# First modulation of the trunk: unsplit float32 products in four column groups instead of split products, with a new opening order

## The chip, the cores and the metric

The kernel runs on one core of one Trainium2 chip. The metric is the device time of one execution in microseconds, the median over repeated executions.

## The reference

A two-layer backbone for a diffusion generator over 256 latent tokens and 256 context tokens of width 1024. Layer 0 mixes tokens with a bidirectional mLSTM, layer 1 with latent attention; each is followed by a gated convolutional feed-forward. Every sub-layer sees its input modulated by six vectors worked out from the condition:

```
m = silu(cond) @ ada_w[i] + ada_b[i]          # (1024) @ (1024, 6*1024), split into six
h = x * (1 + scale) + shift                   # latent tokens: from c, context tokens: from c_ctx
x_m = h @ m_w_up                              # first product of layer 0, (512, 1024) @ (1024, 2048)
```

All of it is float32. The change concerns the first two of the six vectors (shift and scale) of layer 0, for both conditions, and what the first product `x_m` needs of them.

## The kernel before, in words

Large products are made by splitting: a float32 array a is cast on ScalarE to float32r (`hi`), VectorE subtracts (`lo = a - hi`), and TensorE adds three products hi\*hi, hi\*lo, lo\*hi (`mm3`, L405 to L407). Tokens lie along the free axis (512 of them, context first), features on the partitions, in 8 tiles of 128.

The opening (`start_up`) makes the shift and scale of layer 0, modulates the 8 feature tiles, and starts the up projection for its first five column tiles of 128 (`NUP` = 5), which accumulate in five PSUM banks. The rest of the kernel follows from column tile m = 5 on (`w_up`), with weights that a stream loads and splits ahead.

Two lists written out by hand set the order. `LOADS` is the order of the DMAs on SP's queue: `a..` a 128 x 1024 tile of modulation weights (512 KB, 16 in all), `x.` a tile of transposed tokens (256 KB), `w.` a tile of up weights (128 x 640, 320 KB), `s` the small constants. `STEPS` is the order of the work, which is kept as written on TensorE, VectorE and ScalarE:

- `Sgi` splits weight tile i of group g on ScalarE and VectorE (`ada_split`); `Agi` and `Bgi` multiply its high and its low half (`ada_mm`, L487). The stationary operand is `condr`, 4 columns: the high and the low parts of SiLU(c) and SiLU(c_ctx). The result `adar` is a row of 4 partitions.
- `Cg` copies that row out of PSUM on ScalarE (L493), `Tg` transposes it in 128-column pieces to feature-major (`ada_T`, L500), `Og` adds the high and low results and the bias on VectorE into `mod0` (L510, L511).
- `Ek` modulates token tile k, context half on VectorE (L585) and latent half on ScalarE (L587); `Hk` splits the outcome.
- `Wk` splits up weight tile k; `Vkm` adds tile k's contribution to up column tile m, three products of 128x128 by 128x512. There are 40 of these steps.

`GROUPS` says which feature tiles a modulation group holds: 1, 1, 2, 2 and 2. A group of two has products 512 wide, a group of one 256 wide. Ten products on zeros (L627) stand ahead of the first step. `setup` loads the 16 KB with the condition and bias on SP's queue ahead of everything else (L446) and makes `cond` (SiLU, L463) and `condr`.

After the opening the instructions are ordered by the scheduler. The split of column tile 5 goes into a buffer that the up weight tile w3 holds until its last `V3m` step.

Of the kernel before, what the change touches and what calls it, by code (L numbers as in the profile page):

```python
# [7 lines left out]
F32 = mybir.dt.float32  # L8
F32R = mybir.dt.float32r
I32 = mybir.dt.int32  # L10
AF = mybir.ActivationFunctionType
# [38 lines left out]


NUP = 5
GROUPS = ((0, 1), (1, 2), (2, 4), (4, 6), (6, 8))
WARM = 10
LOADS = (
    "a00 a01 a10 a11 a20 a21 x0 w0 x1 a22 a23 w1 s a30 a31 a32 a33 w2 x2 x3 a40 w3 a41 a42 a43 w4 x4 x5 x6 w5 x7 "
    "w6 w7").split()
STEPS = (
# [4 lines left out]
    "V73 V71 V32 V63 V60 V61 V72 V70 V64 V74").split()  # L63

TAIL = {"mout": 4, "aout": 7, "fout1": 6}
WIDE = {"mout": 5, "aout": 7, "fout1": 10}
# [79 lines left out]
def _pack(i):  # L146
# [87 lines left out]

    w0 = np.asarray(i["ada_w"][0]).reshape(8, 128, 6, D)[:, :, 0:2]
    ada0 = []
    for f0, f1 in GROUPS:
        g = w0[..., f0 * 128:f1 * 128].transpose(1, 0, 2, 3).reshape(128, -1)
        ada0 += [g[:, j:j + 1024] for j in range(0, g.shape[1], 1024)]

    up0 = i["m_w_up"][0].reshape(8, 128, -1)[:, :, :NUP * 128]
# [134 lines left out]
class K:  # L376
# [64 lines left out]
    def setup(self):  # L441
        nc, p = self.nc, self.pool
        a = self.a
        self.sm = p.tile([128, a["sm"].shape[1]], F32, name="sm")
        self.sm0 = p.tile([128, NSM0], F32, name="sm0")
        nc.sync.dma_start(self.sm0, a["sm0"])  # L446
        b1 = self.smc("ada_b")[:, 8:16]
        nc.vector.tensor_scalar(b1, b1, 1.0, None, op0=ALU.add)
        jp = p.tile([128, 128], I32, tag="s2", name="jp", bufs=NS)
        nc.gpsimd.iota(jp, pattern=[[1, 128]], base=0, channel_multiplier=-1)  # L450
        self.ident = p.tile([128, 128], F32, name="ident")
        nc.vector.tensor_scalar(self.ident, jp, 0.0, None, op0=ALU.is_equal)
        self.mask = p.tile([128, 2, 128], F32, name="mask")
        nc.vector.tensor_scalar(self.mask[:, 0], jp, 0.0, NEG, op0=ALU.is_gt, op1=ALU.mult)
        nc.vector.tensor_scalar(self.mask[:, 1], jp, 0.0, NEG, op0=ALU.is_lt, op1=ALU.mult)
        self.k1 = p.tile([128, 1], F32, name="k1")
        nc.vector.memset(self.k1, 1.0)
        self.zero = p.tile([128, 512], F32R, tag="s2", name="zero", bufs=NS)
        nc.vector.memset(self.zero.bitcast(F32), 0.0)
        self.keps = p.tile([128, 1], F32, name="keps")  # L460
        nc.vector.memset(self.keps, EPS)
        self.cond = p.tile([128, 8, 2], F32, name="cond")
        nc.scalar.activation(self.cond.rearrange("p a b -> p (a b)"), self.smc("cond"), AF.Silu)  # L463
        self.condr = p.tile([128, 8, 4], F32R, name="condr")
        self.split(self.condr[:, :, 0:2], self.condr[:, :, 2:4], self.cond)
        self.mod0 = p.tile([128, 2, 8, 2], F32, name="mod0")
        self.modc = {(0, c): self.mod0[:, c] for c in range(2)}
        self.gd = {}
        self.adav = p.tile([128, 32], F32, name="adav")
        nc.vector.memset(self.adav, 0.0)  # L470
        for l in range(2):
            for c in (3, 4) if l == 0 else (0, 1, 3, 4):
                self.modc[l, c] = p.tile([128, 8, 2], F32, name="mod%d%d" % (l, c))
            for c in (2, 5):
                self.gd[l, c] = self.dr.tile([2, D], F32, name="gd%d%d" % (l, c))

    def ada_split(self, w):
        hi, lo = [self.pool.tile([128, 1024], F32R, tag="u", name="adas", bufs=NU) for _ in range(2)]
        self.split(hi, lo, w)
        return hi, lo  # L480

    def ada_mm(self, pr, g, i, x, start, stop):

        n = 256 * (GROUPS[g][1] - GROUPS[g][0])
        nk = 1024 // n
        for kk in range(nk):
            self.nc.tensor.matmul(pr[0:4, :n], self.condr[:, i * nk + kk, :], x[:, kk * n:(kk + 1) * n],  # L487
                                  start=start and kk == 0, stop=stop and kk == nk - 1)

    def ada_copy(self, pr, g):  # L490
        r = self.s2("adarow")
        n = 256 * (GROUPS[g][1] - GROUPS[g][0])
        self.nc.scalar.copy(r[0:4, :n], pr[0:4, :n])  # L493
        return r

    def ada_T(self, g, r):
        nf = GROUPS[g][1] - GROUPS[g][0]
        pt = self.ps("adat")
        for i in range(2 * nf):
            self.nc.tensor.transpose(pt[:, 4 * i:4 * i + 4], r[0:4, i * 128:(i + 1) * 128], self.ident[0:4, 0:4])  # L500
        return pt

    def ada_cols(self, g, pt):
        nc = self.nc
        f0, f1 = GROUPS[g]
        nf = f1 - f0
        t = self.tiny(8, "adt")[:, 0:4 * nf].rearrange("p (c f b) -> p c f b", c=2, b=2)
        p = pt[:, 0:8 * nf].rearrange("p (c f b) -> p c f b", c=2, b=4)
        b = self.smc("ada_b").rearrange("p (c f) -> p c f", c=2)[:, :, f0:f1].unsqueeze(3).to_broadcast([128, 2, nf, 2])
        nc.vector.tensor_tensor(t, p[:, :, :, 2:4], b, op=ALU.add)  # L510
        nc.vector.tensor_tensor(self.mod0[:, :, f0:f1, :], p[:, :, :, 0:2], t, op=ALU.add)  # L511

    def ada_bg(self, l, c, k0, k1, nconds):

# [74 lines left out]
    def start_up(self):  # L589
# [10 lines left out]
        for step in LOADS:  # L600
            op, n = step[0], [int(x) for x in step[1:]]
            if op == "a":
                t = raw[step] = self.uf("adaw")
                src = self.a["ada0"][sum(2 * (f1 - f0) for f0, f1 in GROUPS[:n[0]]) + n[1]]
            elif op == "x":
                t = raw[step] = self.s2("xT")
                src = self.a["tokT"][n[0]]
            elif op == "w":
                t = raw[step] = self.pool.tile([128, CW], F32, tag=tag[n[0]][0], name="raw0", bufs=tag[n[0]][1])
                t, src = t[:, :nw], self.a["up0"][n[0]]  # L610
            else:
                t, src = self.sm, self.a["sm"]
            nc.sync.dma_start(t, src)
# [5 lines left out]

        e = mybir.EngineType  # L620
        idle = self.ps("idle")
        rows, parts, hT = {}, {}, {}
        todo = {g: 4 * (f1 - f0) for g, (f0, f1) in enumerate(GROUPS)}
        ps, made = {}, [0] * NUP
        with self.tc.manual_schedule(engines={e.PE, e.DVE, e.Activation}):
            for _ in range(WARM):
                nc.tensor.matmul(idle, self.zero[:, 0:128], self.zero, start=True, stop=True)  # L627
            for step in STEPS:
                op, n = step[0], [int(x) for x in step[1:]]
                g = n[0]  # L630
                if op == "S":
                    parts[g, n[1]] = self.ada_split(raw["a%d%d" % (g, n[1])])
                elif op in "AB":
                    first = g not in rows
                    if first:
                        rows[g] = self.ps("adar")
                    todo[g] -= 1
                    self.ada_mm(rows[g], g, n[1], parts[g, n[1]][op == "B"], first, todo[g] == 0)
                elif op == "C":
                    rows[g] = self.ada_copy(rows[g], g)  # L640
                elif op == "T":
                    rows[g] = self.ada_T(g, rows[g])
                elif op == "O":
                    self.ada_cols(g, rows[g])
                elif op == "E":
                    self.mod_tile(g)
                elif op == "H":
                    h = hT[g] = self.u("hT")
                    self.split(h[:, 0, :], h[:, 1, :], self.xT[g])
                elif op == "W":  # L650
                    if g not in w:
                        w[g] = [self.pool.tile([128, CW], F32R, tag="u", name="w0", bufs=NU) for _ in range(2)]
                    self.split(w[g][0][:, :nw], w[g][1][:, :nw], raw["w%d" % g][:, :nw])
                else:
                    k, m = n
                    if m not in ps:
                        ps[m] = self.ps("up")
                    c = slice(m * 128, (m + 1) * 128)
                    self.mm3(ps[m], (w[k][0][:, c], w[k][1][:, c]), (hT[k][:, 0], hT[k][:, 1]),
                             made[m] == 0, made[m] == 7)  # L660
                    made[m] += 1
        self.hT = [hT[k] for k in range(8)]
        raw = parts = w = w3 = rows = None
        for m in range(NUP):
            self.up_evac(m, ps[m])

# [1351 lines left out]
```

## Time and profile before

| | us |
|---|---|
| median of 3 runs | 1365.69 (1365.69 to 1366.27) |
| span of the profiled execution | 1363.8 |
| TensorE busy in it | 1347.3 |
| VectorE busy | 1073.6 |
| ScalarE busy | 725.3 |
| first up product of the opening starts | 14.90 |
| first product of column tile 5 starts | 53.61 |

The profiled execution is known by its span, from its first to its last instruction; the runs' times also hold what lies around it. Rows of a timeline read: start, length, engine, source line, operation, out<-in with shapes, count, and in square brackets how long the engine was idle before and what ended that. PE is TensorE, PEld its weight loads, DVE VectorE, ACT ScalarE, SPq the DMA queue of SyncE. Grouped rows end with busy time and mean ns of one instruction, then the idle time before them. A TensorE row's length is longer than the distance to the next row's start, since neighbours overlap in the array.

### The profile page before, as it was taken

Reading aid. Unit: us, or ns where it says so; the run is one execution under the profiler, and the core shown is the slowest. Engines: PE = TensorE matmul, PEld = TensorE weight load, DVE = VectorE, ACT = ScalarE, POOL = GpSimd, SP = SyncE. Lnnn points to the kernel's source line nnn. Section 1 sums busy time; section 2 is a strip of 40 time slices with the busy share of each in tenths; the row PEclk is TensorE's granted clock in tenths of the full one; section 3 lists DMA queues with packets and bytes.
Section 4 is the critical chain, followed back from the end, with each engine's and each line's share of the span. In section 5 each row is a group of like instructions: output and inputs, shape, how many; then the busy total and the mean of one; then the engine's idle time right before and its main releaser. Section 6 shows DMA issues by size and latency. Waiting matters only on the chain.

```text
span 1363.8 us, 18639 instructions
## 1 busy us (share of the span) xinstructions
PE 1347.3 (99%) x6605; PEld 1125.5 (83%) x6605; DVE 1073.6 (79%) x1738; ACT 725.3 (53%) x1251; POOL 121.9 (9%) x215
## 2 busy tenths in 40 slices
PE   8999999999999999999999999999999999999997
PEld 5788888888788888888898888888888888888886
DVE  7798656677598696897979978767898789888873
ACT  7765443446544555464643334334557767466660
POOL 0122000010011011030001000000001001000100
PEclk9999999999999999999999999999999999999999
DMA  9788748788666374776627876646998436366750
GB/s 367 273 294 299 272 170 264 228 296 279 216 208 201 101 232 135 249 282 229 210 95 239 301 242 229 219 144 206 307 272 242 142 103 206 114 189 193 257 193 31
DMA packets 92077, 297.60 MB, mean 218 GB/s; under 512 B 12072, under 2 KB 16552, under 8 KB 91984
## 3 DMA queue, kind: packets, MB, share of 16 engines
q1 hardware_dynamic: 62848, 218.52, 48.2%
q0 software_dynamic: 17472, 57.57, 13.5%
q10 hardware_dynamic: 11664, 20.32, 4.1%
q8 instruction: 52, 0.85, 0.2%
q14 instruction: 41, 0.34, 0.1%
HBM read 262.90 MB, written 33.46 MB: 217 GB/s over the span
## 4 chain that ended last, share of the span: by engine, by line
PE 95%; DVE 2%; ACT 1%; DMA 1%; issue 1%; SPq 0%; DVEq 0%; ACTq 0%
PE fin L1354 8%; PE y L406 6%; PE fin L405 6%; PE y L407 6%; PE fin L406 6%; PE fin L407 6%; PE y L405 6%; PE tok L405 6%; PE tok L407 6%; PE tok L406 6%; PE qk L405 4%; PE qk L407 4%; PE qk L406 4%; PE up L406 2%; PE up L405 2%; PE up L407 2%
## 5 line engine op out<-in xcount | busy, mean ns | idle before, releaser
L347 DVE TENSOR_TENSOR w<-raw,w 128x1024 fp32r<-128x1024 f32 (+2 forms) x286 | 343.4, 1203 | 148.6 <-ACT w L344 144.8
L344 ACT CAST w<-raw 128x1024 fp32r<-128x1024 f32 (+2 forms) x286 | 296.7, 1038 | 282.5 <-PE fin L407 78.5
L528 DVE SCALAR_TENSOR_TENSOR junk<-ar,bc 128x1024 f32<-128x1024 f32 x128 | 155.9, 1218 | 3.3 <-ACT bc L570 1.0
L406 PE MATMUL fin<-h,w 128*128 128x512 f32 (+1 forms) x376 | 141.2, 376 | 0.0
L407 PE MATMUL fin<-h,w 128*128 128x512 f32 (+1 forms) x376 | 140.9, 375 | 0.0
L405 PE MATMUL fin<-h,w 128*128 128x512 f32 (+1 forms) x376 | 140.8, 376 | 0.1
L1354 PE MATMUL fin<-h,w 128*128 128x256 f32 (+1 forms) x640 | 111.9, 337 | 0.0
L1354 PEld LDWEIGHTS fin<-h,w 128*128 128x128 f32 x640 | 98.3, 190 | 13.4
L405 PE MATMUL qk<-xc,w 128*128 128x512 f32 x256 | 100.7, 393 | 0.0
L407 PE MATMUL qk<-xc,w 128*128 128x512 f32 x256 | 99.9, 390 | 0.0
L406 PE MATMUL qk<-xc,w 128*128 128x512 f32 x256 | 99.8, 390 | 0.0
L406 PEld LDWEIGHTS fin<-h,w 128*128 128x128 f32 x376 | 70.8, 188 | 13.1 <-DVE h L1208 0.2
L407 PEld LDWEIGHTS fin<-h,w 128*128 128x128 f32 x376 | 70.8, 188 | 12.7
L405 PEld LDWEIGHTS fin<-h,w 128*128 128x128 f32 x376 | 70.6, 188 | 13.0 <-ACT h L1207 0.3
L405 PEld LDWEIGHTS qk<-xc,w 128*128 128x128 f32 x256 | 48.1, 188 | 10.1 <-issue 0.4
L407 PEld LDWEIGHTS qk<-xc,w 128*128 128x128 f32 x256 | 48.1, 188 | 10.0
L406 PEld LDWEIGHTS qk<-xc,w 128*128 128x128 f32 x256 | 48.1, 188 | 9.6
L406 PE MATMUL up<-hT,w 128*128 128x512 f32 x128 | 50.0, 391 | 0.2 <-DVE hT L411 0.2
L405 PE MATMUL up<-hT,w 128*128 128x512 f32 x128 | 50.1, 391 | 0.0
L407 PE MATMUL up<-hT,w 128*128 128x512 f32 x128 | 49.8, 389 | 0.0
L405 PE MATMUL tok<-w,hT 128*128 128x512 f32 x128 | 49.8, 389 | 0.0
L406 PE MATMUL tok<-w,hT 128*128 128x512 f32 x128 | 49.8, 389 | 0.0
(464 smaller groups left out, 3167.1 us busy)
## 6 DMA issues: line engine op xcount, KB each, us to landing
raw<-in_ws SPq DMA_DIRECT2D x282, 512.0 KB, 4.5
ar<-in_adaT SPq DMA_DIRECT2D x80, 512.0 KB, 4.7
adaw<-in_ada SPq DMA_DIRECT2D x16, 512.0 KB, 9.1
t2d<-raw ACTq DMA_DIRECT2D x13, 512.0 KB, 4.8
raw<-t2d SPq DMA_DIRECT2D x13, 512.0 KB, 5.2
raw<-in_ws POOLq DMA_DIRECT2D x13, 512.0 KB, 8.1
zr<-fd ACTq DMA_DIRECT2D x33, 128.0 KB, 4.6
xmd<-xr POOLq DMA_DIRECT2D x16, 256.0 KB, 4.2
```

What stands on the lines that cost most here:

```text
L344: k.nc.scalar.copy(h[:, :cols], src)
L347: k.nc.vector.tensor_sub(l[:, :cols], src, h[:, :cols])
L405: mm(out, w[0], x[0], start=start, stop=False, skip_group_check=on)
L406: mm(out, w[0], x[1], start=False, stop=False, skip_group_check=on)
L407: mm(out, w[1], x[0], start=False, stop=stop, skip_group_check=on)
L528: nc.vector.scalar_tensor_tensor(o, w, 1.0, self.bc[j], op0=ALU.mult, op1=ALU.mult, accum_out=col[:, k, j:j + 1])
L1354: nc.tensor.matmul(ps[:, :n] if x else ps, w[x][:, c], hT(k)[0] if x else both(k), start=i == 0, stop=i == 15)
```

## The change

The modulation weights are no longer split. Each of the 8 feature tiles is a group of its own (`GROUPS` is gone). The condition `cond` is a float32 tile with 32 columns for each of 8 row blocks, of which two are filled and the rest is zero (POOL writes the zeros). For one feature tile, TensorE makes 8 unsplit float32 products, 128x32 by 128x256, four for each weight tile, and puts the four of a weight tile into the four groups of 32 array columns, so that the partial sums come out on partitions 0, 32, 64 and 96. A copy of all 128 partitions goes to SBUF, and two small products with a 0/1 matrix `pick` (128x2) add the four partial sums and turn them to feature-major at once. `O` adds the bias in one operation. There are no `S` and `B` steps, and `STEPS` and `LOADS` are written anew, feature tile by feature tile. The 16 KB with the condition are loaded on ScalarE's queue.

On ScalarE the built order begins: DMA issue of the 16 KB, table load, cast of w0, table load, SiLU of the condition, copy C0. On TensorE it begins: the ten products on zeros, A0, T0, A1, V00, T1, V01 to V04, A2. On SP: a00, a01, w0, a10, a11, x0, x1, w1, and then tile by tile.

```diff
-GROUPS = ((0, 1), (1, 2), (2, 4), (4, 6), (6, 8))
 LOADS = (
-    "a00 a01 a10 a11 a20 a21 x0 w0 x1 a22 a23 w1 s a30 a31 a32 a33 w2 x2 x3 a40 w3 a41 a42 a43 w4 x4 x5 x6 w5 x7 "
-    "w6 w7").split()
+    "a00 a01 w0 x0 a10 a11 x1 w1 a20 a21 x2 w2 a30 a31 x3 w3 a40 a41 x4 w4 a50 a51 x5 w5 s a60 a61 x6 w6 a70 "
+    "a71 x7 w7").split()
 STEPS = (
-    "S00 A00 B00 S01 A01 S10 S11 B01 C0 T0 O0 A10 S20 A11 B11 B10 S21 A21 E0 C1 A20 T1 W0 H0 B20 B21 O1 S22 E1 "
...
-    "B42 B41 A41 H4 A42 S43 W6 V44 A43 B43 V42 H5 V40 W5 V43 C4 T4 W7 O4 V51 E7 E6 V54 V50 V53 H7 V41 H6 V52 V62 "
-    "V73 V71 V32 V63 V60 V61 V72 V70 V64 V74").split()
+    "A0 W0 C0 T0 O0 E0 H0 A1 V00 C1 W1 T1 V01 V02 O1 V03 E1 V04 H1 A2 W2 V10 C2 V11 T2 V12 O2 E2 V13 H2 A3 W3 "
+    "V14 C3 V20 T3 V21 O3 E3 V22 H3 A4 W4 V23 C4 V30 T4 V31 O4 E4 V32 H4 A5 W5 V33 C5 V40 T5 V41 O5 E5 V42 H5 "
+    "V43 A6 W6 V50 C6 V51 T6 V52 O6 E6 V53 H6 A7 W7 V24 C7 V60 T7 V61 O7 E7 V62 H7 V63 V34 V70 V71 V72 V73 "
+    "V44 V54 V64 V74").split()
...
-        nc.sync.dma_start(self.sm0, a["sm0"])
+        nc.scalar.dma_start(self.sm0, a["sm0"])
...
-        self.cond = p.tile([128, 8, 2], F32, name="cond")
-        nc.scalar.activation(self.cond.rearrange("p a b -> p (a b)"), self.smc("cond"), AF.Silu)
-        self.condr = p.tile([128, 8, 4], F32R, name="condr")
-        self.split(self.condr[:, :, 0:2], self.condr[:, :, 2:4], self.cond)
+        self.cond = p.tile([128, 8, 32], F32, tag="s2", name="cond", bufs=NS)
+        nc.gpsimd.memset(self.cond, 0.0)
+        nc.scalar.activation(self.cond[:, :, 0:2], self.smc("cond").rearrange("p (a b) -> p a b", b=2), AF.Silu)
+        self.pick = p.tile([128, 2], F32, name="pick")
+        nc.vector.tensor_reduce(self.pick, self.ident.rearrange("p (j i) -> p i j", i=32)[:, 0:2], axis=AX.X, op=ALU.add)
...
+    def ada_mm(self, pr, ws):
+
+        for x, w in enumerate(ws):
+            for j in range(4):
+                q = slice(32 * j, 32 * j + 32)
+                self.nc.tensor.matmul(pr[q, 0:256], self.cond[:, 4 * x + j, :], w[:, j * 256:(j + 1) * 256],
+                                      start=x == 0, stop=x == 1, tile_position=(0, 32 * j), skip_group_check=True)
+
+    def ada_copy(self, pr):
+        r = self.pool.tile([128, 256], F32, tag="s2", name="adarow", bufs=NS)
+        self.nc.scalar.copy(r, pr[:, 0:256])
         return r
...
+    def ada_T(self, pr, r):
+        for c in range(2):
+            self.nc.tensor.matmul(pr[:, 256 + 2 * c:258 + 2 * c], r[:, c * 128:(c + 1) * 128], self.pick,
+                                  start=True, stop=True, skip_group_check=True)
+
+    def ada_cols(self, f, pr):
+        b = self.smc("ada_b").rearrange("p (c f) -> p c f", c=2)[:, :, f:f + 1].to_broadcast([128, 2, 2])
+        p = pr[:, 256:260].rearrange("p (c b) -> p c b", c=2)
+        self.nc.vector.tensor_tensor(self.mod0[:, :, f, :], p, b, op=ALU.add)
```

More of the change, by code (lines that the diff above doesn't have):

```diff
@@ L236, in _pack @@
     ada0 = []
-    for f0, f1 in GROUPS:
-        g = w0[..., f0 * 128:f1 * 128].transpose(1, 0, 2, 3).reshape(128, -1)
+    for f in range(8):
+        g = w0[..., f * 128:(f + 1) * 128].transpose(1, 0, 2, 3).reshape(128, -1)
         ada0 += [g[:, j:j + 1024] for j in range(0, g.shape[1], 1024)]
@@ L475, in setup @@
                 self.gd[l, c] = self.dr.tile([2, D], F32, name="gd%d%d" % (l, c))
[L477 to L493, printed above, removed]
-        return r
[L496 to L511, printed above, removed]
+    def ada_mm(self, pr, ws):
[4 more added lines that the diff above has]
+                                      start=x == 0, stop=x == 1, tile_position=(0, 32 * j), skip_group_check=True)
@@ L603, in start_up @@
                 t = raw[step] = self.uf("adaw")
-                src = self.a["ada0"][sum(2 * (f1 - f0) for f0, f1 in GROUPS[:n[0]]) + n[1]]
+                src = self.a["ada0"][2 * n[0] + n[1]]
             elif op == "x":
@@ L621, in start_up @@
         idle = self.ps("idle")
-        rows, parts, hT = {}, {}, {}
-        todo = {g: 4 * (f1 - f0) for g, (f0, f1) in enumerate(GROUPS)}
+        rows, adas, hT = {}, {}, {}
         ps, made = {}, [0] * NUP
@@ L630, in start_up @@
                 g = n[0]
[L631 to L638, printed above, removed]
+                if op == "A":
+                    rows[g] = self.ps("adar")
+                    self.ada_mm(rows[g], [raw["a%d%d" % (g, x)] for x in range(2)])
                 elif op == "C":
-                    rows[g] = self.ada_copy(rows[g], g)
+                    adas[g] = self.ada_copy(rows[g])
                 elif op == "T":
-                    rows[g] = self.ada_T(g, rows[g])
+                    self.ada_T(rows[g], adas[g])
                 elif op == "O":
@@ L662, in start_up @@
         self.hT = [hT[k] for k in range(8)]
-        raw = parts = w = w3 = rows = None
+        raw = adas = w = w3 = rows = None
         for m in range(NUP):
```

2 rows, old and new, of the table STEPS are left out of this document.

## The prediction

> **What bounds the kernel now.** I read the page first: the busy shares, then the chain of work that ended last.
>
> ```profile
> span 1363.8 us, 18639 instructions
> ...
> PE 1347.3 (99%) x6605; PEld 1125.5 (83%) x6605; DVE 1073.6 (79%) x1738; ACT 725.3 (53%) x1251; POOL 121.9 (9%) x215
> ...
> PE 95%; DVE 2%; ACT 1%; DMA 1%; issue 1%; SPq 0%; DVEq 0%; ACTq 0%
> ```
>
> TensorE is busy 99% of the span and is 95% of the chain. So a change to the opening is worth exactly what it does to the moment at which TensorE has finished the opening's products; everything behind is shifted as a block. Next, TensorE's timeline of the opening, and the stretch from the first up product to the first product of tile m = 5 (not part of the hand order).
>
> ```profile
> 14.90 0.49 PE L405 MATMUL up<-hT,w 128*128 128x512 f32 x1
> ...
> 17.59 0.40 PE L406 MATMUL up<-hT,w 128*128 128x512 f32 x1
> 17.83 0.39 PE L407 MATMUL up<-hT,w 128*128 128x512 f32 x1
> ...
> 53.61 0.39 PE L405 MATMUL up<-hT,w 128*128 128x512 f32 x1
> ```
>
> The same stretch as a window, for all instructions, for L487 alone (modulation products) and for L500 alone (transposes); the columns are length, TensorE busy (count), weight loads busy (count):
>
> ```profile
> 14.88:53.60 38.72, 38.49 (x173) 26.74 (x173) 30.56 (x46) 29.24 (x43) 0.25 (x1) 1.00 0.91 344
> 14.88:53.60 38.72, 10.96 (x41) 3.23 (x40) 1.00 0.91 344
> 14.88:53.60 38.72, 1.22 (x12) 0.96 (x12) 1.00 0.91 344
> ```
>
> From 14.9 us on TensorE has 38.49 of 38.72 us busy: 120 up products, some 40 modulation products, 12 transposes, without a hole. Starts of neighbours are 0.227 us apart (17.59 to 17.83, and 40 steps of three products make 120 x 0.227 = 27.2 us); a row's 0.39 us is that plus a tail of 0.17 us which the next product covers. So the modulation holds about 11.3 us of this stretch, and the opening ends at **53.6 us**.
>
> ScalarE, VectorE and the DMA queue tell what sets the 14.9.
>
> ```profile
> 0.74 1.28 ACT L463 ACT_TABLE_LOAD   x1 [0.74 <-PEq L2008]
> 2.54 0.21 ACT L463 ACTIVATE cond<-sm 128x16 f32<-128x16 f32 x1 [0.51 <-DMA sm<-in_sm]
> ...
> 5.08 1.05 ACT L410 CAST adas<-adaw 128x1024 fp32r<-128x1024 f32 x1 [2.09 <-DMA adaw<-in_ada]
> 6.38 1.05 ACT L410 CAST adas<-adaw 128x1024 fp32r<-128x1024 f32 x1 [0.25 <-DMA adaw<-in_ada]
> ...
> 12.46 0.60 ACT L587 ACTIVATE xT<-xT,mod 128x256 f32<-128x256 f32 x1
> 12.96 0.35 ACT L493 COPY adarow<-adar 4x256 f32<-4x256 f32 x1
> 13.21 0.72 ACT L410 CAST w<-raw 128x640 fp32r<-128x640 f32 x1
> 14.23 0.62 ACT L410 CAST hT<-xT 128x512 fp32r<-128x512 f32 x1 [0.29 <-DVE xT L585]
> ```
>
> ```profile
> 11.35 0.16 DVE L511 TENSOR_TENSOR mod<-adat,adt 128x4 f32<-128x4 f32 x1
> 11.43 2.38 DVE L411 TENSOR_TENSOR adas<-adaw,adas 128x1024 fp32r<-128x1024 f32 x2
> 13.73 0.41 DVE L585 TENSOR_SCALAR xT<-xT,mod 128x256 f32<-128x256 f32 x1
> ```
>
> ```profile
> 0.75 0.38 SPq L446 DMA_DIRECT2D sm<-in_sm  x1
> 1.18 3.08 SPq L613 DMA_DIRECT2D adaw<-in_ada  x6
> ```
>
> The reader is to see one 512 KB tile landing each 1.3 us (5.08, 6.38), and a first modulation ready at 11.5 whose use waits until 13.73, since VectorE first makes two more low halves (2.38 us).
>
> **The change part by part.**
>
> *Splits removed.*
>
> ```profile
> L411 DVE TENSOR_TENSOR adas<-adaw,adas 128x1024 fp32r<-128x1024 f32 x16 | 19.4, 1224 | 4.8 <-ACT adas L410 4.4 <-DMA raw<-in_up 0.3
> L410 ACT CAST adas<-adaw 128x1024 fp32r<-128x1024 f32 x16 | 16.6, 1048 | 4.0 <-DMA adaw<-in_ada 3.9
> ```
>
> 16 casts (16.6 us of ScalarE) and 16 subtractions (19.4 us of VectorE) go. Behind 14.9 us they lie beside a full TensorE, so there they are worth nothing. Ahead of it they could bring the first up product forward; what is late next there decides (below).
>
> *Modulation products (A).* The nearest rows are eight 256-column products of the old form, and the load of a 32-column operand.
>
> ```profile
> 7.44 1.09 PE L487 MATMUL adar<-adas,condr 128*4 128x256 f32 x8 [0.62 <-DVE adas L411]
> ```
>
> ```profile
> L853 PEld LDWEIGHTS gates<-xc,w 128*32 128x32 f32 x32 | 3.5, 109 | 3.8
> ```
>
> There are now 8 float32 products a feature tile, 64 in all. In the changed instruction stream each of them stands as two pairs of weight load and product, the two halves of the stationary operand, one behind the other on the same column group: 16 pairs a tile. The moving weights are not split, and a fp32r pass drops a remainder (that is why the old kernel subtracts one), so I estimate two passes over 256 columns for each, which is what one 512-column product streams: 0.227 us. If one pass did, it would be 0.116 us ((1.09 - 0.28) / 7: eight products less the last one's 0.28 us, which is 0.116 and the tail). No column groups occur in the trace. Bounds for a tile: four groups abreast and one pass each, 4 x 0.116 = 0.46 us; nothing overlapped and each load exposed, 16 x (0.227 + 0.109) = 5.4 us. Between: TensorE starts products in order (every row of its timeline), and the second half of a product must wait for the first on its own group. So the second half of one group can run only beside the first half of the next: 16 halves in 9 slots, 9 x 0.227 = **2.05 us**. That is also nearest to the row of the old form (8 x 0.227 = 1.82 us for the two raw tiles of a feature tile), and I take it.
>
> The Trainium skill ("TensorE: Matmul & The Clock Gate", Part 3) says that products in different column groups run concurrently, starting about 4 ns apart, and gives 2.38x for three groups. No run here shows it yet. By that speed-up on 16 halves of 0.227 us a tile would cost about 1.5 us, an estimate; in my sum this would be 3 us less in the dense part.
>
> *Change of array form.* Each A stands between 128-wide products. Bounds for entering or leaving: 0, and the uncovered tail plus an uncovered load (0.17 + 0.19 us, the load by the first row of the fence on loads below). I take the tail alone, 0.17, so 0.34 us a tile.
>
> *Small products (T).* Two float32 products with a 128-column stationary operand, so four pairs a tile, for two transposes.
>
> ```profile
> 22.08 0.41 PE L500 MATMUL adat<-ident,adarow 4*128 4x4 f32 x4
> 22.42 0.62 PE L487 MATMUL adar<-adas,condr 128*4 128x512 f32 x2
> ```
>
> ```profile
> L405 PEld LDWEIGHTS up<-hT,w 128*128 128x128 f32 x62 | 11.6, 188 | 3.8 <-ACT hT L410 0.5 <-issue 0.2
> ...
> L500 PEld LDWEIGHTS adat<-ident,adarow 4*128 4x128 f32 x16 | 1.3, 136 | 3.0 <-ACT adarow L493 1.7 <-ACT w L410 0.5 <-ACT adas L410 0.5
> ```
>
> Below: 0.17 us (half of the four transposes' 0.34, from 22.08 to 22.42). Above: four loads and tails end to end, 4 x (0.19 + 0.17) = 1.4 us. Nearest row: four transposes in 0.34 us; their loads are shorter (136 against 188 ns), so I take 0.34 x 188 / 136 = 0.47, rounded to 0.5 us.
>
> *Start.* The condition vector's DMA leaves SP's queue, so the first tiles are issued 0.43 us earlier (1.18 to 0.75): a00 lands at 4.65, a01 at 5.95, w0 (320 KB, 0.8 us) at 6.75. But on ScalarE the cast of w0 now stands ahead of Silu, and a second table load between them. ScalarE takes them in order: 6.75 + 0.72 + 1.28 + 0.21 = 8.96, and only then may A0 start, at 9.05 (the old first one waited only for a00's cast, 5.08 + 1.05). Queued behind that wait are every copy, E and H of the opening. Then: A0 to 11.1, tail 11.27, copy 0.35 to 11.65, T0 0.5 + 0.2 to 12.35, O0 0.16 to 12.55, E0 0.60 to 13.15, H0 0.62 to 13.75. Meanwhile TensorE does A1, from 12.15 with 0.17 + 2.05 to 14.4. The first up product starts at **14.5**: what the removed splits gain is given back by the late Silu and by A1.
>
> *Sum.* 14.5 + 27.2 (up products) + 6 x 2.05 (A2 to A7) + 6 x 0.34 + 7 x 0.5 (T1 to T7) = 59.5 us, against 53.6: **+5.9 us**.
>
> *Costed at nothing.* DMA: a feature tile's 1,600 KB take 4.0 us to land; TensorE spends 3.4 + 2.05 + 0.34 + 0.5 = 6.3 us on it, so after the first two tiles the data is there; without this cover the last tile, landing near 36.5 us, would set an end near 45 us. sm moves back in the queue, its first user is behind the opening. POOL's memset and the pick reduction end before 6 us. The C, O, E, H chain of a tile (about 2 us) lies beside five up steps (3.4 us). Split of up tile 5 (1.0 + 1.2 us) may start after V34, eight steps (5.4 us) ahead of the end. Behind the opening the order on TensorE is unchanged; on the other engines it changes for some 15 splits and evacuations, with TensorE as cover.
>
> The time: the medians lie 1.9 us above the profiled span (1365.69 against 1363.8), which I leave as it is. 1365.7 + 5.9 = **1371.6 us**.
>
> **The rivals.**
>
> 1. *The column groups do not overlap at all.* A is 16 x 0.227 = 3.64 us: first up product 17.7, end 17.7 + 27.2 + 21.8 + 2.0 + 3.5 = 72.2, +18.6: **1384.3 us**. For it: no row shows two products at once. Against: nothing.
>
> 2. *Faster: the halves run four abreast* (or need one pass). A is 4 x 0.227 = 0.91 us: A0 ends at 10.15, the first up product starts at 12.65, end 12.65 + 27.2 + 5.5 + 2.0 + 3.5 = 50.9, -2.7: **1363.0 us**; without the cost of changing form 1361.0. It decides below A = 1.3 us, where the end comes out at 53.6. For it: nothing else in the sum hinders it. Against: products start in order.
>
> 3. *The array's clock falls at the start.*
>
> ```profile
> 1.49 3.87 PE L627 MATMUL idle<-zero 128*128 128x512 f32 x10 [1.49 <-DVE adav L470]
> ```
>
> The ten idle products took 3.87 us, 0.39 us apart instead of 0.227, so the array begins slower and speeds up on work. TensorE would now be idle from 5.4 (1.49 + 3.87) to 9.05 us. If it slows again, A0, T0 and A1 double: +2.2 + 0.5 + 2.05, about +5 us: **1376.5 us**. The Trainium skill (same page, Part 1) says that after about 3.4 us of idle the clock is halved until it has been busy as long; the trace's slow first products agree, the halving after idle no row here shows.
>
> 4. *The change does not do what it says:* the splits stay. The new order of instructions has none, so no chance is given.
>
> **How the numbers follow.** Forecast (pairs) 0.48, with its own range from the bounds: form change 0 and T 0.17 give about 1367, 0.36 a side and T 1.4 about 1381. Rival 1: 0.25. Rival 2: 0.18. Rival 3: 0.09. The range 1362.5 to 1384.5 holds all but the fast end of rival 2 and, where loads are exposed too, the slow end of rival 1. About 0.2% (2.7 us) is what a measurement can tell from no change. Rival 2 lies on that edge: 0.12 faster, 0.06 same; the forecast's low end gives 0.06 more to same. Slower 0.76.
>
> **What would show it.** First up product near 14.5 and the first one of m = 5 near 59.5. The A rows: a tile's 16 products 2.05 us, starts two at a time (right), 0.227 apart singly (rival 1), or four within a few ns (rival 2). Silu after 8.7 us, behind a second table load. T rows: four in 0.5 us. Granted clock below 1.00 in the first 15 us (rival 3). The forecast is wrong if TensorE has holes behind the first up product, for then a chain and not its work bounds the opening.

## The result, and the profile after

The changed kernel takes 1368.12 us (median of 20 runs, 1365.35 to 1370.93) beside 1365.99 us for the kernel before on the same chip (20 runs, 1365.43 to 1368.12): a ratio of 1.0016, 95% interval 1.0009 to 1.0023. It is 2.1 us slower; +5.9 was forecast. The profiled execution's span grew by 2.3 us. From the page of the changed kernel, the span, the busy times and the chain that ended last by engine:

```profile
span 1366.1 us, 18744 instructions
...
PE 1348.2 (99%) x6669; PEld 1127.6 (83%) x6669; DVE 1055.0 (77%) x1720; ACT 710.6 (52%) x1238; POOL 122.2 (9%) x216
...
PE 93%; DMA 2%; ACT 2%; DVE 2%; issue 1%; ACTq 0%; SPq 0%; DVEq 0%
```

VectorE lost 18.6 us of work and ScalarE 14.7, TensorE gained 0.9, and TensorE is still the chain. TensorE's timeline of the opening, changed kernel (the up products are now L403 to L405, A is L481, T is L491):

```profile
1.49 4.64 PE L612 MATMUL idle<-zero 128*128 128x512 f32 x10 [1.49 <-DVE adav L469]
8.91 1.07 PE L481 MATMUL adar<-adaw,cond 128*32 128x256 f32 x16 [2.78 <-ACT cond L462]
10.47 1.02 PE L491 MATMUL adar<-pick,adarow 128*128 128x2 f32 x4 [0.49 <-ACT adarow L486]
11.42 1.94 PE L481 MATMUL adar<-adaw,cond 128*32 128x256 f32 x16
13.29 0.79 PE L403 MATMUL up<-hT,w 128*128 128x512 f32 x1
...
17.40 0.63 PE L404 MATMUL up<-hT,w 128*128 128x512 f32 x1
17.83 0.63 PE L405 MATMUL up<-hT,w 128*128 128x512 f32 x1
...
20.36 0.39 PE L405 MATMUL up<-hT,w 128*128 128x512 f32 x1
20.68 1.07 PE L481 MATMUL adar<-adaw,cond 128*32 128x256 f32 x16
21.68 0.50 PE L403 MATMUL up<-hT,w 128*128 128x512 f32 x1
22.01 0.40 PE L404 MATMUL up<-hT,w 128*128 128x512 f32 x1
...
23.17 0.51 PE L491 MATMUL adar<-pick,adarow 128*128 128x2 f32 x4
23.54 0.48 PE L403 MATMUL up<-hT,w 128*128 128x512 f32 x1
23.86 0.40 PE L404 MATMUL up<-hT,w 128*128 128x512 f32 x1
...
54.69 0.39 PE L403 MATMUL up<-hT,w 128*128 128x512 f32 x1
```

Three things are to be seen. A tile's modulation (20.68) is over in 1.07 us with its tail, half the forecast. But the same work at 11.42 took 1.94, T at 10.47 took 1.02 against 0.51 at 23.17, and up products at 17.40 and 17.83 start 0.43 us apart instead of 0.227: everything between 10.05 and 20.3 runs at half pace. And tile m = 5 starts at 54.69, 1.08 us later than before.

The granted clock, in two windows of the changed kernel (columns: length, TensorE busy (count), weight loads, VectorE, ScalarE, POOL, granted clock, DMA share, GB/s):

```profile
6.64:10.05 3.41, 1.07 (x16) 0.42 (x16) 0.83 (x1) 2.19 (x4) 0.00 (x0) 1.00 1.03 409
10.05:20.30 10.25, 9.83 (x38) 7.13 (x39) 4.12 (x8) 4.43 (x8) 0.00 (x0) 0.50 1.03 405
```

In 3.41 us TensorE had 1.07 us of work; then the clock is at half for 10.25 us, though TensorE is busy for 9.83 of them. ScalarE's timeline tells why there was so little work:

```profile
6.61 0.72 ACT L408 CAST w<-raw 128x640 fp32r<-128x640 f32 x1 [4.14 <-DMA raw<-in_up]
7.35 1.28 ACT L462 ACT_TABLE_LOAD   x1
8.64 0.22 ACT L462 ACTIVATE cond<-sm 128x16 f32<-128x16 f32 x1
```

The SiLU comes behind the cast of w0 and a second table load, so TensorE is idle from 6.13 (1.49 + 4.64) to 8.91 us.

The other 1.2 us of the span (2.3 - 1.08) lie far behind the opening, near 990 us, where TensorE waits for streamed weights. TensorE's waits of the changed kernel, and then of the kernel before:

```profile
PE y L404 <- DVE w L345: 1.0, 1, 1.0
...
PE y L403 <- ACT w L342: 0.3, 1, 0.3
```

```profile
PE y L406 <- DVE w L347: 0.4, 1, 0.4
```

### The profile page after: what moved, and what is told of

It reads as the page before. It is cut to its first block, busy times and chain, and to the rows that moved or that the text cites. A ratio compares the mean times of both kernels' runs of the same rounds, so it can differ in the third digit from the quotient of the medians.

```text
span 1366.1 us, 18744 instructions
## 1 busy us (share of the span) xinstructions
PE 1348.2 (99%) x6669; PEld 1127.6 (83%) x6669; DVE 1055.0 (77%) x1720; ACT 710.6 (52%) x1238; POOL 122.2 (9%) x216
## 4 chain that ended last, share of the span: by engine, by line
PE 93%; DMA 2%; ACT 2%; DVE 2%; issue 1%; ACTq 0%; SPq 0%; DVEq 0%
PE fin L1334 8%; PE fin L404 6%; PE fin L403 6%; PE fin L405 6%; PE tok L403 6%; PE tok L405 6%; PE tok L404 6%; PE y L404 5%; PE y L405 5%; PE y L403 5%; PE qk L403 4%; PE qk L405 4%; PE qk L404 4%; PE up L403 2%; PE up L404 2%; PE up L405 2%
## 5 line engine op out<-in xcount | busy, mean ns | idle before, releaser
L405 PE MATMUL fin<-h,w 128*128 128x512 f32 (+1 forms) x376 | 140.9, 375 | 0.0
L403 PE MATMUL fin<-h,w 128*128 128x512 f32 (+1 forms) x376 | 140.8, 376 | 0.1
L403 PE MATMUL qk<-xc,w 128*128 128x512 f32 x256 | 100.6, 393 | 0.0
L405 PE MATMUL qk<-xc,w 128*128 128x512 f32 x256 | 99.9, 390 | 0.0
L403 PEld LDWEIGHTS fin<-h,w 128*128 128x128 f32 x376 | 70.5, 188 | 13.2 <-ACT h L1187 0.3
L405 PEld LDWEIGHTS fin<-h,w 128*128 128x128 f32 x376 | 70.8, 188 | 12.6
L403 PEld LDWEIGHTS qk<-xc,w 128*128 128x128 f32 x256 | 48.1, 188 | 10.0 <-issue 0.4
L405 PEld LDWEIGHTS qk<-xc,w 128*128 128x128 f32 x256 | 48.1, 188 | 9.9
L403 PE MATMUL up<-hT,w 128*128 128x512 f32 x128 | 52.6, 411 | 0.0
L404 PE MATMUL up<-hT,w 128*128 128x512 f32 x128 | 51.2, 400 | 0.0
L405 PE MATMUL up<-hT,w 128*128 128x512 f32 x128 | 50.9, 398 | 0.0
L403 PE MATMUL tok<-w,hT 128*128 128x512 f32 x128 | 49.8, 389 | 0.0
```

The lines of the kernel that those rows point to most:

```text
L403: mm(out, w[0], x[0], start=start, stop=False, skip_group_check=on)
L404: mm(out, w[0], x[1], start=False, stop=False, skip_group_check=on)
L405: mm(out, w[1], x[0], start=False, stop=stop, skip_group_check=on)
```

## The experiments

The theory from these rows: two rivals came true together. Four column groups run abreast, which makes the opening some 2 to 3 us faster than before, and the clock falls in the hole ahead of A0, which takes that back and more. The rival theory: the products still overlap only in part, and what is lost is the chain of the first tile. A summary first; "behind" is the span less the start of tile m = 5, and each ratio is against the kernel before as it ran beside that kernel (its medians there lie between 1365.99 and 1366.42):

| kernel | first up product | tile m = 5 | behind | median us | ratio (95%) |
|---|---|---|---|---|---|
| before | 14.90 | 53.61 | 1310.2 | 1365.99 | |
| changed | 13.29 | 54.69 | 1311.4 | 1368.12 | 1.0016 (1.0009 to 1.0023) |
| filled start | 13.26 | 51.73 | 1310.4 | 1364.20 | 0.9985 (0.9976 to 0.9994) |
| first hole filled | 12.92 | 51.48 | 1310.6 | 1364.34 | 0.9989 (0.9980 to 0.9998) |
| SiLU first | 11.30 | 49.87 | 1310.7 | 1365.40 | 0.9993 (0.9984 to 1.0001) |
| SiLU first, filled | 11.92 | 50.44 | 1310.6 | 1362.93 | 0.9977 (0.9968 to 0.9986) |
| the same, x0 early | 11.01 | 50.99 | 1311.6 | 1363.99 | 0.9982 (0.9974 to 0.9991) |
| one column group | 18.98 | 74.39 | 1311.6 | 1387.87 | 1.0159 (1.0140 to 1.0177) |
| other group orders | 14.32 | 59.89 | 1312.1 | 1372.39 | 1.0042 (1.0022 to 1.0062) |
| no idle products | 14.27 | 55.84 | 1312.7 | 1368.35 | 1.0010 (1.0001 to 1.0019) |
| before, no idle products | 16.50 | 55.02 | 1310.7 | 1367.53 | 1.0010 (1.0001 to 1.0019) |

**Filled start.** Products on zeros keep TensorE at work up to the first up product; nothing else moves.

```diff
-WARM = 10
+WARM = 24
-    "A0 W0 C0 T0 O0 E0 H0 A1 V00 ...
+    "A0 I2 W0 C0 T0 O0 E0 H0 A1 I3 V00 ...
+                if op == "I":
+                    for _ in range(g):
+                        nc.tensor.matmul(idle, self.zero[:, 0:128], self.zero, start=True, stop=True)
```

> The changed kernel with TensorE kept busy on zeros until the first up product: 24 idle products at the start instead of 10, two more behind A0, three behind A1. Theory (the halved clock between 10.1 and 20.3 us costs about half of the 9.8 us that TensorE is busy there): the granted clock stays at 1.00 once it has risen, the up products start near 12.6 us at full speed, and the time is about 5 us under the changed kernel's, 1363 us, so some 2.7 us under the kernel before. Rival (the clock costs nothing, since the start waits for transfers and for the other engines; the 2 us are the price of the small products and of changing the array's form): the time stays at 1368 us or rises by the idle products, up to 1370 us.

Its timeline, and the same two windows:

```profile
9.35 1.07 PE L481 MATMUL adar<-adaw,cond 128*32 128x256 f32 x16
...
11.44 1.07 PE L481 MATMUL adar<-adaw,cond 128*32 128x256 f32 x16
...
13.26 0.39 PE L403 MATMUL up<-hT,w 128*128 128x512 f32 x1
```

```profile
6.64:10.05 3.41, 3.41 (x29) 2.35 (x27) 0.83 (x1) 2.23 (x3) 0.00 (x0) 1.00 1.03 412
10.05:20.30 10.25, 10.05 (x76) 6.62 (x68) 4.12 (x8) 4.72 (x9) 0.00 (x0) 1.00 1.03 403
```

A0 starts later than in the changed kernel (9.35 against 8.91), and the first up product at the same time (13.26 against 13.29). Yet tile m = 5 comes 3.0 us earlier, since the clock stays at 1.00. More work on TensorE, less time: the clock was the loss. All 11 runs lie within 1.1 us (1363.68 to 1364.79) with a mean granted clock of 0.998 or 0.999. Of the changed kernel's 20 runs, 16 have 0.993 to 0.996. The other four (0.998, 0.999) are no faster, 1367.90 to 1370.93; what such a mean can hide, the run with other group orders shows below.

**First hole filled.** Eight more products ahead of A0 and none behind it.

```diff
-WARM = 10
+WARM = 18
```

> The changed kernel with 18 idle products at the start instead of 10, and none later: only the hole ahead of A0 is filled (to about 7.5 us). Theory (the hole ahead of A0 lets the clock fall): like the kernel with all holes filled, 1364.2 us, clock at 1.00 behind its rise, and the runs lie within some 1.5 us. Rival (the whole thin stretch up to the first up product lets it fall): like the changed kernel, 1368.1 us, with runs spread over 5 us.

The profiled execution kept the clock, and tile m = 5 came at 51.48. But the runs spread over 4.7 us (1363.21 to 1367.86), and the three slowest, 1366.16 and up, are the three with a mean clock of 0.997 or 0.996. So the hole ahead of A0, cut from 2.78 to 1.09 us, is most of it. What is left of it, or the holes behind A0, probably still lets the clock fall in some executions; no profile shows one of those.

**SiLU first.** The SiLU goes ahead of the cast of w0, which also saves the second table load.

```diff
-        nc.scalar.activation(self.cond[:, :, 0:2], self.smc("cond").rearrange("p (a b) -> p a b", b=2), AF.Silu)
...
         with self.tc.manual_schedule(engines={e.PE, e.DVE, e.Activation}):
+            nc.scalar.activation(self.cond[:, :, 0:2], self.smc("cond").rearrange("p (a b) -> p a b", b=2), AF.Silu)
```

> The changed kernel with SiLU of the condition ahead of the cast of w0 on ScalarE (one table load instead of two), nothing else. Theory (clock): A0 starts near 6.3 us instead of 8.9; the first up product then waits for x0 and H0 and starts near 11.5 us. TensorE's hole behind the idle products shrinks to some 0.2 us, but it has little to do until 11 us, so the clock may or may not fall: 1361.5 us if it stays up, about 1366 us if it falls. Rival (the late SiLU is what costs the 2 us, and the clock nothing): 1366 us, with the first up product 1.8 us earlier.

TensorE's timeline in this run, and a row of ScalarE's, the latent half of E0:

```profile
6.38 1.53 PE L480 MATMUL adar<-adaw,cond 128*32 128x256 f32 x16 [0.25 <-ACT cond L610]
...
11.30 0.50 PE L403 MATMUL up<-hT,w 128*128 128x512 f32 x1 [1.28 <-ACT hT L408]
```

```profile
10.00 0.60 ACT L572 ACTIVATE xT<-xT,mod 128x256 f32<-128x256 f32 x1 [1.64 <-DMA xT<-in_tokT]
```

A0 comes 2.5 us earlier and the first up product 2.0. In the profiled execution the clock held and the span was 1360.6 us. The chain now waits for x0, which lands at 10.00, and TensorE waits 1.28 us behind it. In other runs the mean clock is lower and the time goes with it: from 1362.41 us at 0.998 to 1367.69 at 0.995. Against the kernel before, the median gains nothing that can be told from no change.

**SiLU first, filled.** Both edits: `WARM = 12`, and the order `A0 I2 W0 C0 T0 I4 O0 E0 H0 A1 I3 V00`.

> Both: SiLU first, and idle products to fill TensorE's holes up to the first up product (12 at the start, 2 behind A0, 4 behind T0, 3 behind A1). Theory (clock): the clock stays up, the first up product starts near 11.3 us, the opening ends near 49 us, 4.5 us before that of the kernel before: 1361.5 us. Rival (the clock costs nothing): no faster than SiLU first alone, about 1366 us.

The same two views of this run:

```profile
6.91 1.13 PE L480 MATMUL adar<-adaw,cond 128*32 128x256 f32 x16
...
11.92 0.43 PE L403 MATMUL up<-hT,w 128*128 128x512 f32 x1
```

```profile
10.54 0.60 ACT L572 ACTIVATE xT<-xT,mod 128x256 f32<-128x256 f32 x1 [2.05 <-DMA xT<-in_tokT]
```

x0 landed half a microsecond later than in the run before, and the first up product came 0.6 later. The fillers cost it at most 0.1 us: it starts 0.13 us behind the end of H0's cast (11.79), against 0.05 in the run before. Why x0 landed later is open. All 11 runs have a mean clock of 0.998 or 0.999. This version beats both kernels: 0.9977 against the one before.

**The same, x0 early.** In addition SP's queue keeps the written order, with x0 ahead of w0 (in the runs above x0 was issued behind w0, a10 and a11), V00 and V01 stand ahead of A1, and the three fillers behind A1 go.

```diff
-    "a00 a01 w0 x0 a10 ...
+    "a00 a01 x0 w0 a10 ...
-    "A0 W0 C0 T0 O0 E0 H0 A1 V00 C1 W1 T1 V01 V02 O1 V03 ...
+    "A0 I2 W0 C0 T0 I4 O0 E0 H0 V00 V01 A1 C1 W1 V02 T1 V03 O1 ...
```

> SiLU first and idle products (12 at the start, 2 behind A0, 4 behind T0), and the DMA queue kept in the written order with x0 ahead of w0 (a00, a01, x0, w0), and V00 and V01 ahead of A1. If the start of the up products is now set by the landing of x0 (theory, from the wait of SiLU first: TensorE sat idle for 1.3 us for H0), the first up product moves from 11.9 to about 10.2 us, and the time from 1362.9 to about 1361.3 us. Rival: the start is set by the chain copy, small products, bias, modulation and split, whatever lands when; then 1362.9 us again.

ScalarE's timeline in this run, and O0 on VectorE:

```profile
7.74 0.73 ACT L408 CAST w<-raw 128x640 fp32r<-128x640 f32 x1 [1.36 <-DMA raw<-in_up]
8.37 0.37 ACT L485 COPY adarow<-adar 128x256 f32<-128x256 f32 x1
9.70 0.60 ACT L572 ACTIVATE xT<-xT,mod 128x256 f32<-128x256 f32 x1 [0.97 <-DVE mod L496]
```

```profile
9.50 0.16 DVE L496 TENSOR_TENSOR mod<-adar,sm 128x4 f32<-128x4 f32 x1 [0.18 <-PE adar L490]
```

E0 (9.70) no longer waits for x0 but for O0, O0 for T0, and T0 for the copy C0, which stands behind the cast of w0 on ScalarE; and w0 now lands later. So the theory holds for the first part of the way, and then the rival's chain sets the start: the first up product comes at 11.01, 0.9 us earlier than without this edit, where 1.7 was expected. A1 now stands behind it, in the dense part, where it costs its full 1.2 us. Tile m = 5 comes 0.55 us later: no gain.

**One column group.** All eight products of a tile go to group 0, one accumulation; the copy and the small products then take 32 rows.

```diff
-                q = slice(32 * j, 32 * j + 32)
-                self.nc.tensor.matmul(pr[q, 0:256], self.cond[:, 4 * x + j, :], w[:, j * 256:(j + 1) * 256],
-                                      start=x == 0, stop=x == 1, tile_position=(0, 32 * j), skip_group_check=True)
+                self.nc.tensor.matmul(pr[0:32, 0:256], self.cond[:, 4 * x + j, :], w[:, j * 256:(j + 1) * 256],
+                                      start=x + j == 0, stop=x + j == 4, tile_position=(0, 0), skip_group_check=True)
```

> The changed kernel with all eight products of a feature tile on the first column group, one behind the other, adding up there; the copy and the small products then take 32 rows instead of 128. It gives the price of one half product. Theory A (each half streams its 256 columns twice, 0.213 us, and the changed kernel ran four groups abreast): 16 halves take 3.4 us a tile instead of 0.87, the opening is some 18 us longer: 1386 us. Theory B (each half streams once, 0.107 us, and only two groups ran abreast): 1.7 us a tile, some 6 us longer: 1374 us.

A tile's row in this run, then the modulation products alone in the first 0.03 us of a tile, here and in the changed kernel (columns: length, TensorE busy (count), weight loads busy (count), clock, DMA share, GB/s):

```profile
23.35 3.64 PE L480 MATMUL adar<-adaw,cond 128*32 128x256 f32 x16
```

```profile
23.35:23.38 0.03, 0.03 (x1) 0.03 (x2) 1.00 0.36 137
```

```profile
20.68:20.71 0.03, 0.03 (x4) 0.03 (x6) 1.00 1.04 410
```

The 16 halves follow one another at (3.64 - 0.38) / 15 = 0.217 us here, 0.38 being the length of a single one. So each half takes the time of two passes over 256 columns, as the estimate and theory A had it. In the changed kernel four are in the array after 0.03 us, 3.64 / 1.07 = 3.4 times as fast with the tail. The column groups are worth 20 us to this change (1387.87 against 1368.12).

The clock fell here too, but for a shorter time. The row of the long window:

```profile
10.05:20.30 10.25, 9.80 (x40) 4.86 (x38) 1.46 (x4) 2.57 (x5) 0.00 (x0) 0.84 1.04 406
```

A mean of 0.84 over 10.25 us is some 3.3 us at half, against all 10.25 in the changed kernel. In those 3.3 us TensorE had nothing but A0's halves, one behind the other (A0 runs from 9.10 for 5.33 us).

**Other group orders.** Why four, where the forecast had two? Tiles 2 and 6 use the groups in the order 0 0 1 1 2 2 3 3, tiles 3 and 7 as 0 1 0 1 0 1 0 1, tile 4 as 0 0 0 0 1 1 1 1; tiles 0, 1 and 5 stay.

```diff
+        if f in (2, 6):
+            order = [(x, j) for j in range(4) for x in range(2)]
+        elif f in (3, 7):
+            group = lambda x, j: j % 2
+        elif f == 4:
+            group = lambda x, j: x
```

> Edit: the modulation products of feature tiles 0, 1 and 5 stay as changed (groups 0 1 2 3 0 1 2 3); tiles 2 and 6 go to the same groups in the order 0 0 1 1 2 2 3 3; tiles 3 and 7 use two groups in turn (0 1 0 1 0 1 0 1); tile 4 uses two groups in blocks (0 0 0 0 1 1 1 1). The changed kernel's rows show 16 half products starting four at a time, 0.216 us apart; the run on one group shows 16 in a row, 0.216 us apart. Open is how four can start together if the two halves of a product stand one behind the other and must follow each other on their own group. Theory 1, TensorE looks ahead to products on free groups: the order does not matter, only the number of groups. Tiles 2 and 6: 16 / 4 = 4 steps of 0.216, 0.87 us, as before; tiles 3, 7 and 4: 16 / 2 = 8 steps, 1.73 us. First product of column tile 5 then 3 x 0.86 = 2.6 us later than in the changed kernel, 57.3. Theory 2, products start strictly in the order of the program and only the halves are interleaved (first halves of a run of products on different groups, then their second halves): tiles 3 and 7 still 8 steps, 1.73 us; tiles 2 and 6, where neighbours share a group, 8 steps or more, 1.7 to 2.2 us; tile 4 some 15 steps, 3.2 us. First product of column tile 5 then 2 x 0.86 + 2 x 0.86 to 1.3 + 2.4 = 5.8 to 6.8 us later, near 61. The two halves being able to run at once on one group is excluded by the run on one group.

Tiles 1 to 5 in its timeline, and the first moments of tiles 2, 3 and 4 as above; the last row is tile 4 again, 0.88 us on:

```profile
12.46 1.93 PE L490 MATMUL adar<-adaw,cond 128*32 128x256 f32 x16
...
21.59 1.09 PE L490 MATMUL adar<-adaw,cond 128*32 128x256 f32 x16
...
26.04 1.92 PE L490 MATMUL adar<-adaw,cond 128*32 128x256 f32 x16
...
31.60 2.81 PE L490 MATMUL adar<-adaw,cond 128*32 128x256 f32 x16
...
38.05 1.07 PE L490 MATMUL adar<-adaw,cond 128*32 128x256 f32 x16
```

```profile
21.59:21.64 0.05, 0.04 (x4) 0.05 (x6) 1.00 1.07 410
26.03:26.06 0.03, 0.03 (x2) 0.03 (x2) 1.00 0.61 239
31.60:31.63 0.03, 0.03 (x1) 0.03 (x2) 1.00 0.56 222
32.48:32.52 0.04, 0.04 (x3) 0.03 (x2) 1.00 1.88 749
```

Neighbours on the same group (tile 2) cost 0.02 us: four run at once all the same. Two groups in turn make 8 steps of 0.216 (1.92 with the tail). Two groups in blocks make 12, not 8 and not 15: (2.81 - 0.38) / 11 = 0.22. That is what comes out if products for a free group overtake waiting ones, but only so far: with 8 halves for each group and 12 steps, four run two abreast, so group 1 starts beside group 0's fifth half, past three that wait. The last row shows it: four steps on, three halves are in the array, where one behind the other leaves two at most. Group 1 was not held up by its weight tile a41: that was issued before 14.5 us, and no such load of this run took more than 8.1 us to land. Tile 2 fits too: the last group starts at once, past three that wait on each of the other groups. So theory 1 holds with a limit of three waiting halves per group; the three is inferred from these two orders alone. Theory 2, starts strictly in the order of the program, is out. The expected 57.3 for tile m = 5 became 59.89. Tile 4's four extra steps are 0.9 of the difference, and 1.0 is there before the first up product already (14.32 against 13.29). Most of the last 0.7 is T, which in the three tiles with two groups works on 64 rows and holds TensorE for 0.53 us (29.48 to 30.01) instead of 0.36.

The 1.0 is the clock again. The view of windows says 1.00 for this run's whole start:

```profile
10.00:13.40 3.40, 2.91 (x28) 1.55 (x24) 0.57 (x2) 0.94 (x2) 0.00 (x0) 1.00 1.03 412
```

But A1, inside and behind this window, took 1.93 us, as at half clock. The view counts the clock as 1.00 until the first recorded change, and in this run the pace first doubles near 21 us. The spacing of equal products is the better witness. So a mean of 0.998 or 0.999 does not show that the start ran at full clock; the four runs of the changed kernel with such means fit that, since they are as slow as the rest, but none of them was profiled.

**No idle products,** in the changed kernel and in the one before: `WARM = 0`.

> The changed kernel without any idle products at the start. Theory (the clock rises only after a stretch of about 3.4 us that is nearly full): it stays at half until some 3 to 7 us behind the first up product, as in the changed kernel, and only A0 and the first small products are slower: 1368 to 1369.5 us. Rival (the ten idle products keep the array at speed for part of the start): 1371 us or more.

> The kernel before without its ten idle products. Theory: the modulation products begin at half clock, TensorE is nearly full from 10.5 us on, the clock rises near 14 to 17 us, and the time is 1 to 3 us longer, 1367 to 1369 us. Rival (the clock of the start costs nothing): 1366 us.

The changed kernel's A0, without idle products:

```profile
9.04 1.93 PE L481 MATMUL adar<-adaw,cond 128*32 128x256 f32 x16 [9.04 <-ACT cond L462]
```

It runs at half pace from its first product and reaches tile m = 5 at 55.84, 1.15 us later than with the ten; the medians are 0.2 us apart, with runs that spread over 5 us: no difference, as the theory had it. The kernel before loses 1.4 us to tile m = 5 without them (55.02 against 53.61), 1.1 of its median, which fits the theory. In the changed kernel the ten products mostly buy a clock that is lost again at 10 us.

## Why the prediction was right or wrong

The time lies in the range; the size was off, +5.9 us forecast against +2.1. That the direction came out right is luck: with the clock held, four abreast make the kernel faster (0.9985 and 0.9989 above). What made it slower is the clock, which the sum did not hold, and 1.2 us behind the opening, which nothing in the prediction foresaw.

- **What bounds the kernel:** right for the opening: there is no hole behind the first up product, and its end passes on to the span. The opening gave +1.08. "Everything behind is shifted as a block" holds only to within some 2.5 us. The rest of the span behind the opening is 1310.2 to 1312.7 us over the eleven kernels, and it doesn't follow the opening: 1310.4 to 1310.7 with four that filled the start or hurried it, 1311.6 with a fifth of those. The +1.2 of the changed kernel's profiled execution is such a difference. What sets it was not tried.
- **Splits removed, worth nothing by themselves; DMA, chain and POOL hidden:** right. 33 us less on VectorE and ScalarE show in no time.
- **Start:** A0 was put at 9.05 and came at 8.91, behind the second table load, for the reason given. The first up product was put at 14.5 and came at 13.29. A1 ahead of it, put at 2.05, took 1.94, but because of the clock; with the first hole filled it took 1.07 and the up product came at 12.92.
- **Modulation products: the step that failed.** "16 halves in 9 slots, 9 x 0.227 = **2.05 us**" was measured as four steps of 0.216, 0.87 us (1.07 with the tail). The price of a half was right (0.217 on one group). The premise "TensorE starts products in order" was not: it was read from rows in which every product used the whole array, and products for other groups overtake those that wait. Rival 2 was this case, with 0.91. In the dense part that is 6 x 1.18 = 7.1 us less than forecast.
- **Change of form:** 0.34 us a tile was taken. By the rows, a product ahead of A takes 0.32 instead of 0.227 (20.36 to 20.68), A 1.00 instead of 0.87 (20.68 to 21.68), the one behind it 0.33 instead of 0.227 (21.68 to 22.01): 0.09 + 0.13 + 0.10 = 0.32. Right.
- **T:** 0.5 was taken; 0.37 (23.17 to 23.54) and 0.09 more in the product behind it (0.32 instead of 0.23) make 0.46. Right.
- **The clock, rival 3:** given 0.09, and it happened. It was priced as +5 alone, since only A0, T0 and A1 were thought to double. It lasts until 20.3, so up products double as well: the terms at full clock, 27.2 + 6 x (0.87 + 0.32) + 7 x 0.46 = 37.6 us, stand against 41.40 measured (13.29 to 54.69), and half of the 7.0 us up to 20.3 is 3.5; 0.3 stays open. With the first hole filled, tile m = 5 came 3.2 us earlier.
- **Rivals as alternatives:** the second fault. Rivals 2 and 3 have different causes and could be true together; no chance stood for both. Rival 2 forecast -2.7, and the first hole filled, where the clock held, gives -2.1 at tile m = 5 (51.48 against 53.61). Rival 2's -2.7 and 3.5 for the clock would have made +0.8, against the opening's +1.08.

On the order of products, the Trainium skill ("TensorE: Matmul & The Clock Gate", Part 3) says that products in different column groups run concurrently, starting about 4 ns apart. The windows above agree that they run concurrently, with four in the array within 0.03 us. The same part of the Trainium skill says that products start and end strictly in program order; tiles 2 and 4 of the run with other group orders differ, and the measurement decides.

On the clock, the same page of the Trainium skill (Part 1) says that it is judged in free-running windows of about 3.4 us, and falls after an idle one. The fall at 10.05 comes at the end of a window in which TensorE worked for 1.07 of 3.41 us, so here little work was enough, without a whole window of idleness. By the Trainium skill's rule there that one busy window restores the clock, it should have been back near 17 us, since the up products are dense from 13.29; it came at 20.3. The run on one column group agrees with that rule: some 3.3 us of A0's halves, and the clock was back.

Why it stayed low for so long in the changed kernel was not settled. There, without idle products and with other group orders, the pace doubled at 20.3, 21.4 to 21.8 and near 21 us, each time over 4 us behind the end of T1 (15.55, 16.54 and 16.59), with nothing but up products 0.43 us apart in the last 3.4 of them. So the small products of T, and the wider starts around them (0.54 to 0.59 us), may count as too little work; that is argued, and no run takes them out.

## What to carry to other kernels

Price the clock with every hole that an edit opens or widens near the start: here 1.07 us of work in a 3.41 us stretch cost over 3 us later on, and 19 more products on zeros in the holes turned a loss of 0.16% into a gain of 0.15%. Rivals with different causes can come true together, so give the pair a chance and a price too. Read a rule such as "products start in order" only as far as its rows reach: rows of full-width products say nothing about products in separate column groups.

## What the runs showed of the hardware

- An unsplit float32 product of 128x32 by 128x256 is two halves of 0.217 us each; four groups run them four abreast (1.07 us for 16 with the tail, 3.64 on one group).
- A product for a free column group overtakes waiting ones, by these orders with up to three halves waiting for a group; a longer run on one group holds the others up (12 steps instead of 8, 2.81 us against 1.92).
- The clock fell with TensorE at work for 31% of a 3.41 us window, and stayed at half for 10.25 us, in which it was busy for 9.83. With 2.31 us of work in the same window (first hole filled) it held; with serial halves on one column group it was back after some 3.3 us.
- The view of the clock reads 1.00 until its first recorded change, even where equal products take twice as long.
